# First mixer blocks summed in two halves, six blocks in step with the modulation, heads between the later halves, and the mixer's loads moved further ahead

## The chip, the cores and the metric

The kernel runs on one core of a Trainium2 chip. The metric is the device time of one execution in microseconds; the median of three executions of the kernel before is 3031.77 us (3027.84 to 3035.3). Everything is one program on five engines that run side by side: TensorE (PE, with its weight loads PEld), VectorE (DVE), ScalarE (ACT), GpSimd (POOL) and SyncE (SP, which only issues transfers).

## What is computed

The reference is a block with a mixer and a product-key lookup, followed by two further layers. The change lies in the mixer, and here in its first part:

```python
mod = silu(c) @ w_ada + b_ada                 # six vectors: shift1, scale1, gate1, shift2, scale2, gate2
h = rms_norm(x, norm1_gain) * (1 + scale1) + shift1
p = h @ w_in                                  # [256, 2048] @ [2048, ...], K = 2048 in 16 chunks of 128
# fq, fk, fv, ff, mq, mk, mv, mo, mi, mf = split(p)
# fox_attention: 8 heads of 128 over 256 rows, logits + F[t] - F[s], causal softmax
# mlstm_chunkwise: 4 heads of 256 on silu(conv(mq, mk)), gates from mi, mf
y = concat([fox_out, mlstm_out]) @ w_out
```

All of it is fp32: a product is made of three matmuls of split operands (high by high, high by low, low by high), so each loaded weight block of 128 x 1024 is split by an ACT cast (`hi`, line 233) and a DVE subtraction (`lo`, line 234) before PE may use it.

## The kernel before

x has 256 rows; its transpose `hT` holds 16 chunks of 128 channels. A weight load (`load`, lines 228 to 235) fetches 512 KB into a buffer `raw` by a transfer that SP issues, and splits it into `hi` and `lo`. In the mixer there are six `raw` buffers and three each of `hi` and `lo`. A block of `gemm_a` (lines 260 to 273) is 512 columns wide: eight loads, each followed by 12 matmuls of 512 columns (lines 249 to 251). `gemm_b` (lines 275 to 287) gives the transposed product, with lines 257 and 258. Sums of both go to the PSUM tag `mm` (four buffers, two to a block); everything else in PSUM uses the tag `at` (four buffers).

**The loop over the modulation** (lines 477 to 486) has eight rounds of two chunks. A round loads four 1 MB blocks of `w_ada` (`aw`, eight buffers), reduces each on DVE to a column of shift or scale (`ada_dot`, line 373), modulates and transposes two chunks of x into `hT`, and runs one load each of the first three blocks of `w_in` (q, k and v of the first four attention heads): 36 matmuls. The sums of these blocks stay in PSUM through all eight rounds: two tiles each for q, k (tag `mm`) and v (tag `at`).

**The attention part** (lines 495 to 507) goes twice over q, k, v of four heads. `fox_qk` normalises and transposes q and k; `mx_gates` (once) makes the forget gates and sends them by two transfers of POOL's queue through DRAM to all partitions (`spread`, lines 624 to 631: `FB` for the attention heads, `MB` for the mLSTM heads). `fox_head` (lines 715 to 740) is a chain: two logit matmuls (723), POOL's addend `fadd` (724), a DVE row maximum (707), ACT's exponential (709), a DVE scaling (727), three transposes (731), an ACT copy, the product with v (736 to 738), the split of the result. The second pair's three blocks (24 loads) are written behind the first four heads and fill PE while these run.

**Then** the pools of the attention are closed, the pools of the mLSTM part are opened on the same memory, and `mx_conv` runs `gemm_b` twice for each of q and k; its sums leave PSUM through `joined` (lines 300 to 303) into tiles `cx` of the new pools. The rest of `w_ada` for the mixer (48 blocks, `ada_beside`, two buffers) is loaded and reduced beside these products, one generator step for each load of a product.

The order of each engine is made by the framework's list scheduler from program order. `soon()` moves a load, its cast and its subtraction ahead by `OFFM` places in that order (100); inside the modulation loop this is off (`self.ahead`). Buffers of one tag are handed out in program order.

Of the kernel before, what the change touches and what calls it, by code (L numbers as in the profile page):

```python
# [9 lines left out]
F32 = mybir.dt.float32  # L10
# [9 lines left out]
P = 128  # L20
S = 256
D = 2048
NK = 16
# [6 lines left out]
X2=1  # L30
X3=0
PR=2
OFFM = 100
OFFP = 130
OFFA = 100
OFFB = 80
# [128 lines left out]
class K:  # L165
# [91 lines left out]
        mm(out, wh, x, start=start, stop=False)  # L257
        mm(out[:, 0, :], wl, x[:, 0, :], start=False, stop=stop)  # L258

    def gemm_a(self, xT, w, off, nk, width, out=None, part=None):  # L260

        xh, xl = xT[:2]
        out = out or [self.ps([P, width], "mm") for _ in range(2)]
        per = max(1, min(nk, SUB // width))
        for c0 in part or range(0, nk, per):
            hi, lo = self.load(w, off + c0 * width, per * width)
            for c in range(c0, c0 + per):
                s = slice((c - c0) * width, (c - c0 + 1) * width)
                for t in range(2):
                    tt = slice(t * P, t * P + P)  # L270
                    self.mm3(out[t], xh[:, c, tt], xl[:, c, tt], hi[:, s], lo[:, s], c == 0, c == nk - 1)
            self.step()
        return out

# [172 lines left out]
    def mixer(self, x_in, xd):  # L447

        nc, tc, a = self.nc, self.tc, self.a
        wctx = ExitStack()  # L450
        self.wpools(wctx, 2, 1, 1, "right")
        ctx = ExitStack()
        hT = self.xt_tiles(self.pool(ctx, "mxh", 1))
        sm = self.pool(ctx, "mxs", 1)
        mk = sm.tile([P, 7 * P], F32, name="mxmask")
        self.tri = mk[:, 0:P]
        self.cmask = mk[:, P:4 * P]
        self.cmask_t = mk[:, 4 * P:7 * P]
        pre = ExitStack()
        xp = self.pool(pre, "mxx", 1)  # L460
        x = xp.tile([P, 2, D], F32, name="x0")
# [10 lines left out]
        self.row_scale(xp, ss, r)  # L472
        off = NK * 16
        W = NK * 512
        first = [[self.ps([P, 512], tag) for _ in range(2)] for tag in ("mm", "mm", "at")]
        self.ahead = False
        for c in range(0, NK, 2):
            ws = [(vec, k, self.ada_load(vec, k)) for vec in range(2) for k in (c, c + 1)]
            for w in ws:
                self.ada_dot(*w)  # L480
            for vec in range(2):
                self.ada_fix(vec, c, 2)
            part = range(c, c + 2, 2)
            self.modulated(x, r, 0, hT, part)
            for i in range(3):
                self.gemm_a(hT, a["w_in"], off + i * W, NK, 512, first[i], part)
        self.ahead = True
        pre.close()
        oT = self.xt_tiles(self.pool(wctx, "mxo", 1, "right"))
        self.ada_open(wctx, 2, "right")  # L490
        self.side = self.ada_beside((2, 4, 3))
        fox = ExitStack()
        at = fox.enter_context(tc.tile_pool(name="mxa", bufs=2))
        a1 = fox.enter_context(tc.tile_pool(name="mxb", bufs=1))
        for g in range(2):
            qT = self.fox_qk(a1, at, hT, off, "fq", -(128.0 ** -0.5), first[0])
            kT = self.fox_qk(a1, at, hT, off + W, "fk", 1.0, first[1])
            ps = first[2] or self.gemm_a(hT, a["w_in"], off + 2 * W, NK, 512)
            v = at.tile([P, 2, 512], F32, tag="fv", name=self.nm("fv"))
            for t in range(2):  # L500
                nc.scalar.copy(v[:, t, :], ps[t])
            first = [None] * 3
            if g == 0:
                gates = self.mx_gates(sm, a1, hT)
            off += 3 * W
            for h in range(4):
                self.fox_head(at, gates, qT, kT, v, g * 4 + h, h, oT)
        fox.close()
        at = fox.enter_context(tc.tile_pool(name="mxc", bufs=2))
        a1 = fox.enter_context(tc.tile_pool(name="mxd", bufs=1))  # L510
        pend = []
        for g in range(2):
            qT = self.mx_conv(at, hT, off, g * 4, "mq")
# [74 lines left out]
    def mx_gates(self, p, fox, hT):  # L588
# [32 lines left out]
            mm(t[:, P:S], lf[:, 1], self.tri, start=False, stop=True)  # L621
            return t

        def spread(pool, x, name):

            n = x.shape[0]
            d = self.dp.tile([1, n * S], F32, name=name + "d")
            nc.gpsimd.dma_start(d.rearrange("o (n q) -> (o n) q", n=n), x)
            out = pool.tile([P, n, S], F32, name=name)
            nc.gpsimd.dma_start(out.rearrange("p n q -> p (n q)"), d.to_broadcast([P, n * S]))  # L630
            return out


        FL = fox.tile([8, S], F32, name="gFL")
        nc.vector.tensor_copy(FL, rows(lf[:, :, 0:8]))
        FB = spread(fox, FL, "gFB")
        fr = fox.tile([4, S], F32, name="gfr")
        nc.vector.tensor_copy(fr, rows(lf[:, :, 8:12]))
        ir = self.ps([4, S])
# [3 lines left out]
        nc.vector.tensor_sub(ar, ir, fr)  # L643
        M = fox.tile([4, S], F32, name="gM")
        nc.vector.tensor_tensor_scan(M, ar, ar, 0.0, op0=OP.max, op1=OP.max)
        negM = fox.tile([4, S], F32, name="gnegM")
        nc.vector.tensor_scalar(negM, M, -1.0, None, op0=OP.mult)
        MB = spread(p, negM, "gMB")
        negm = fox.tile([4, S], F32, name="gnegm")
        nc.vector.tensor_sub(negm, negM, fr)  # L650
        pm = self.ps([P, 2, 4])
# [6 lines left out]
    def head_norm(self, pool, ps, nh, hd, out, dim, rs=None):  # L658


        nc = self.nc
        ss = pool.tile([P, 2, nh], F32, tag="hn_ss", name=self.nm("hss"))
        for t in range(2):
            sq = pool.tile([P, nh * hd], F32, tag="hn_sq", name=self.nm("hsq"))
            nc.scalar.activation(sq, ps[t][:, :nh * hd], AF.Square, scale=1.0 if rs is None else rs[:, t:t + 1])
            nc.vector.tensor_reduce(ss[:, t, :], sq.rearrange("p (h d) -> p h d", h=nh), axis=AX.X, op=OP.add)
        r = pool.tile([P, 2, nh], F32, tag="hn_r", name=self.nm("hr"))
        self.rsqrt(r, ss, 1.0 / dim)
        if rs is not None:
            nc.vector.tensor_mul(r, r, rs.unsqueeze(2).to_broadcast([P, 2, nh]))  # L670
        for t in range(2):
            nc.vector.tensor_mul(
                out[:, t, :].rearrange("p (h d) -> p h d", h=nh),
                ps[t][:, :nh * hd].rearrange("p (h d) -> p h d", h=nh),
                r[:, t, :].unsqueeze(2).to_broadcast([P, nh, hd]))

    def fox_qk(self, a1, at, hT, off, gname, scale, ps):

        nc = self.nc
        ps = ps or self.gemm_a(hT, self.a["w_in"], off, NK, 512)  # L680
        n = a1.tile([P, 2, 512], F32, tag="fqn", name=self.nm("fqn"))
        self.head_norm(at, ps, 4, P, n, P)
        g = self.col(gname)
        if scale != 1.0:
            gs = at.tile([P, 1], F32, tag="gs", name=self.nm("gs"))
            nc.vector.tensor_scalar(gs, g, scale, None, op0=OP.mult)
            g = gs
        out = at.tile([P, 4, S], F32, tag="t" + gname, name=self.nm("fT"))
        for h in range(0, 4, 2):
            t = self.ps([P, 2, S])  # L690
            for i in range(2):
                for k in range(2):
# [767 lines left out]
```

## Time and profile before

| | us |
|---|---|
| median of three executions | 3031.77 |
| profiled execution | 3031.14 |
| its span in the trace | 3029.4 |
| PE busy in the span | 2929.3 (97%) |
| DVE busy | 2275.2 (75%) |
| ACT busy | 1665.4 (55%) |
| from the start to the last matmul of the modulation loop | 142.4 |
| to the end of the last attention head | 268 |
| to the end of the mixer, about | 540 |

Matmul records overlap, since PE takes the next one before the last has drained; a busy PE is therefore not a PE at its peak, and the distance between two starts is what a matmul costs. The mixer is the first sixth of the span.

### The profile page before, as it was taken

Reading aid. Unit: us, or ns where it says so; the run is one execution under the profiler, and the core shown is the slowest. Engines: PE = TensorE matmul, PEld = TensorE weight load, DVE = VectorE, ACT = ScalarE, POOL = GpSimd, SP = SyncE. Lnnn points to the kernel's source line nnn. Section 1 sums busy time; section 2 is a strip of 40 time slices with the busy share of each in tenths; the row PEclk is TensorE's granted clock in tenths of the full one; section 3 lists DMA queues with packets and bytes.
Section 4 is the critical chain, followed back from the end, with each engine's and each line's share of the span. In section 5 each row is a group of like instructions: output and inputs, shape, how many; then the busy total and the mean of one; then the engine's idle time right before and its main releaser. Section 6 shows DMA issues by size and latency. Waiting matters only on the chain.

```text
span 3029.4 us, 41563 instructions
## 1 busy us (share of the span) xinstructions
PE 2929.3 (97%) x14698; PEld 2441.4 (81%) x14698; DVE 2275.2 (75%) x3863; ACT 1665.4 (55%) x2696; POOL 194.1 (6%) x228
## 2 busy tenths in 40 slices
PE   5899999899999999999999999999999999999998
PEld 4578888688888888888688878887878888888877
DVE  6888985799789999656765677777688865666664
ACT  4455654444555555454444456666567755655662
POOL 0021000000000000532700000000000000000000
PEclk9899999899999999999999999999999999999999
DMA  9888996675666666776766666666544466555555
GB/s 399 335 313 316 329 342 207 253 284 179 197 193 216 218 215 219 254 237 227 250 195 190 193 196 190 194 193 197 181 133 136 136 207 196 167 175 170 165 166 160
DMA packets 172870, 660.45 MB, mean 218 GB/s; under 512 B 20071, under 2 KB 21107, under 8 KB 159731
## 3 DMA queue, kind: packets, MB, share of 16 engines
q1 hardware_dynamic: 152640, 604.70, 60.0%
q0 software_dynamic: 10368, 37.24, 3.6%
q10 hardware_dynamic: 9654, 15.85, 1.6%
q8 instruction: 115, 1.88, 0.3%
q14 instruction: 93, 0.76, 0.1%
HBM read 632.54 MB, written 25.18 MB: 217 GB/s over the span
## 4 chain that ended last, share of the span: by engine, by line
PE 90%; DVE 5%; ACT 3%; issue 1%; DMA 1%; ACTq 0%; POOL 0%; DVEq 0%; SPq 0%
PE ps L257 23%; PE ps L250 17%; PE ps L249 17%; PE ps L251 17%; PE ps L258 12%; DVE aw L373 2%; DVE lo L234 2%; ACT hi L233 1%; PE ps L862 1%; PE ps L335 0%; PE ps L359 0%; PE ps L1126 0%; ACT v L440 0%; PE ps L992 0%; DMA sB<-in_crow_dram 0%
## 5 line engine op out<-in xcount | busy, mean ns | idle before, releaser
L234 DVE TENSOR_TENSOR lo<-raw,hi 128x1024 fp32r<-128x1024 f32 x962 | 1191.0, 1241 | 515.4 <-ACT hi L233 426.0
L233 ACT CAST hi<-raw 128x1024 fp32r<-128x1024 f32 x962 | 1001.0, 1044 | 692.7 <-PE ps L251 258.0
L257 PE MATMUL ps<-xT,hi 128*128 128x512 f32 (+1 forms) x3104 | 1105.8, 398 | 17.5 <-ACT hi L233 10.5
L258 PE MATMUL ps<-xT,lo 128*128 128x256 f32 (+1 forms) x3104 | 874.6, 283 | 2.0 <-DVE lo L234 1.8
L257 PEld LDWEIGHTS ps<-xT,hi 128*128 128x128 f32 (+1 forms) x3104 | 582.2, 188 | 150.7 <-ACT hr L317 12.0
L258 PEld LDWEIGHTS ps<-xT,lo 128*128 128x128 f32 (+1 forms) x3104 | 585.6, 189 | 7.8 <-DVE lo L234 3.9
L249 PE MATMUL ps<-hi,xT 128*128 128x512 f32 x1152 | 463.8, 404 | 15.0 <-ACT xT L441 11.8
L250 PE MATMUL ps<-lo,xT 128*128 128x512 f32 x1152 | 463.2, 402 | 2.8 <-DVE lo L234 2.5
L251 PE MATMUL ps<-hi,xT 128*128 128x512 f32 x1152 | 462.9, 402 | 0.0
L250 PE MATMUL ps<-lo,wh 128*128 128x512 f32 x1024 | 402.8, 393 | 7.5 <-DVE lo L234 7.5
L249 PE MATMUL ps<-hi,wh 128*128 128x512 f32 x1024 | 403.0, 394 | 1.2 <-ACT wh L306 1.0
L251 PE MATMUL ps<-hi,wl 128*128 128x512 f32 x1024 | 400.2, 392 | 1.3 <-DVE wl L307 1.2
L306 ACT CAST wh<-R 128x256 fp32r<-128x256 f32 x384 | 155.4, 406 | 307.8 <-PE ps L250 301.2
L249 PEld LDWEIGHTS ps<-hi,xT 128*128 128x128 f32 x1152 | 220.9, 192 | 65.4 <-ACT xT L441 13.2
L250 PEld LDWEIGHTS ps<-lo,xT 128*128 128x128 f32 x1152 | 221.7, 192 | 53.2 <-DVE lo L234 5.3
L251 PEld LDWEIGHTS ps<-hi,xT 128*128 128x128 f32 x1152 | 220.8, 192 | 50.3 <-DVE xT L442 0.5
L307 DVE TENSOR_TENSOR wl<-R,wh 128x256 fp32r<-128x256 f32 x384 | 168.3, 440 | 100.2 <-ACT wh L306 99.1
L373 DVE CUSTOM_DVE_ANT_0 aw<-aw,sB 128x2048 f32<-128x2048 f32 x96 | 220.0, 2305 | 25.2 <-ACT sB L360 20.2
L250 PEld LDWEIGHTS ps<-lo,wh 128*128 128x128 f32 x1024 | 192.4, 188 | 55.5 <-DVE lo L234 14.7
L251 PEld LDWEIGHTS ps<-hi,wl 128*128 128x128 f32 x1024 | 191.9, 188 | 45.9 <-DVE wl L307 3.5
L249 PEld LDWEIGHTS ps<-hi,wh 128*128 128x128 f32 x1024 | 192.5, 188 | 43.7 <-ACT wh L306 2.0
L877 POOL TENSOR_TENSOR R<-R,gld 128x256 f32<-128x256 f32 (+1 forms) x96 | 111.1, 1171 | 51.6 <-DMA gld<-gd 51.1
(369 smaller groups left out, 2367.6 us busy)
## 6 DMA issues: line engine op xcount, KB each, us to landing
raw<-in_down_dram SPq DMA_DIRECT2D x256, 512.0 KB, 3.6
raw<-in_up_dram SPq DMA_DIRECT2D x256, 512.0 KB, 3.6
aw<-in_w_ada_dram SPq DMA_DIRECT2D x96, 1024.0 KB, 7.9
raw<-in_b_in_dram SPq DMA_DIRECT2D x128, 512.0 KB, 3.5
raw<-in_w_in_dram SPq DMA_DIRECT2D x112, 512.0 KB, 6.0
raw<-in_a_in_dram SPq DMA_DIRECT2D x49, 512.0 KB, 3.5
raw<-in_w_out_dram SPq DMA_DIRECT2D x32, 512.0 KB, 4.2
raw<-in_w_query_dram SPq DMA_DIRECT2D x32, 512.0 KB, 5.6
```

The source lines that it names most:

```text
L233: self.nc.scalar.copy(hi[:, :n], raw)
L234: self.nc.vector.tensor_sub(lo[:, :n], raw, hi[:, :n].bitcast(F32))
L249: mm(out, lh, rh, start=start, stop=False)
L250: mm(out, lh, rl, start=False, stop=False)
L251: mm(out, ll, rh, start=False, stop=stop)
L257: mm(out, wh, x, start=start, stop=False)
L258: mm(out[:, 0, :], wl, x[:, 0, :], start=False, stop=stop)
L306: self.nc.scalar.copy(hi, src)
L307: self.nc.vector.tensor_sub(lo, src, hi.bitcast(F32))
L373: nc.vector.tensor_tensor_reduce(out=w, in0=w, in1=self.sB, scale=1.0, scalar=0.0, op0=OP.mult, op1=OP.add, accum_out=out)
L862: mm(ps[:, k, :], o2[:, i + k, :], o1[:, i + k].rearrange("p a n -> p (a n)"), start=True, stop=True)
L877: nc.gpsimd.tensor_mul(d, d, st[:, cuts[i] - n0:cuts[i + 1] - n0, :])
```

## The change

Three things move. The first three blocks of `w_in` are summed in two halves: rounds 0 to 3 make chunks 0 to 7, whose sums ACT copies into a new tile `half` in SBUF (12 KB per partition). Rounds 4 to 7 then run six loads each: chunks 8 to 15 of the second three blocks, and chunks 0 to 7 of the same blocks from the `hT` that is already there, so that q, k, v of heads 4 to 7 are complete with the loop. What is left, chunks 8 to 15 of the first three blocks (12 loads), is run behind the gates, one block each ahead of heads 4, 5 and 6; DVE adds each to its `half`. Then q and k of heads 0 to 3 are normalised, and heads 7, 0, 1, 2, 3 follow. `OFFM` goes from 100 to 250. To make room, the mixer has five `raw` buffers, the broadcast of `MB` moves into the mLSTM's pool behind the attention, `negM` shares the tile of `M`, and the square buffer `hn_sq` of `head_norm` has one buffer everywhere (two before in the two later layers).

```diff
-OFFM = 100
+OFFM = 250
...
-    def gemm_a(self, xT, w, off, nk, width, out=None, part=None):
+    def gemm_a(self, xT, w, off, nk, width, out=None, part=None, ends=None):
+        a, b = ends or (0, nk - 1)
...
-                    self.mm3(out[t], xh[:, c, tt], xl[:, c, tt], hi[:, s], lo[:, s], c == 0, c == nk - 1)
+                    self.mm3(out[t], xh[:, c, tt], xl[:, c, tt], hi[:, s], lo[:, s], c == a, c == b)
...
-        self.wpools(wctx, 2, 1, 1, "right")
+        self.wpools(wctx, 1, 1, 1, "right")
...
+        half = sm.tile([P, 3, 2, 512], F32, name="half")
...
-        first = [[self.ps([P, 512], tag) for _ in range(2)] for tag in ("mm", "mm", "at")]
+        first = None
...
             self.modulated(x, r, 0, hT, part)
+            g = c // 8
+            if c % 8 == 0:
+                first = [[self.ps([P, 512], tag) for _ in range(2)] for tag in ("mm", "mm", "at")]
             for i in range(3):
-                self.gemm_a(hT, a["w_in"], off + i * W, NK, 512, first[i], part)
+                self.gemm_a(hT, a["w_in"], off + (3 * g + i) * W, NK, 512, first[i], part, (8, -1) if g else (0, 7))
+            for i in range(3 * g):
+                b = range(c - 8, c - 6, 2)
+                self.gemm_a(hT, a["w_in"], off + (3 + i) * W, NK, 512, first[i], b, (-1, 7))
+            if c == 6:
+                for i in range(3):
+                    for t in range(2):
+                        nc.scalar.copy(half[:, i, t, :], first[i][t])
...
-        for g in range(2):
-            qT = self.fox_qk(a1, at, hT, off, "fq", -(128.0 ** -0.5), first[0])
-            kT = self.fox_qk(a1, at, hT, off + W, "fk", 1.0, first[1])
-            ps = first[2] or self.gemm_a(hT, a["w_in"], off + 2 * W, NK, 512)
...
-            if g == 0:
-                gates = self.mx_gates(sm, a1, hT)
-            off += 3 * W
-            for h in range(4):
-                self.fox_head(at, gates, qT, kT, v, g * 4 + h, h, oT)
+        qkv = fox_qkv(first)
+        gates = self.mx_gates(sm, a1, hT)
+        rest = []
+        for i in range(3):
+            ps = self.gemm_a(hT, a["w_in"], off + i * W, NK, 512, None, range(8, NK, 2), (8, NK - 1))
+            for t in range(2):
+                nc.vector.tensor_add(half[:, i, t, :], ps[t], half[:, i, t, :])
+            rest.append([half[:, i, t, :] for t in range(2)])
+            self.fox_head(at, gates, *qkv, 4 + i, i, oT)
+        old, qkv = qkv, fox_qkv(rest)
+        self.fox_head(at, gates, *old, 7, 3, oT)
+        for h in range(4):
+            self.fox_head(at, gates, *qkv, h, h, oT)
+        off += 6 * W
...
+        gates["MB"] = gates["MB"](a1)
...
-            sq = pool.tile([P, nh * hd], F32, tag="hn_sq", name=self.nm("hsq"))
+            sq = pool.tile([P, nh * hd], F32, tag="hn_sq", name=self.nm("hsq"), bufs=1)
```

`fox_qkv(ps)` is the old body of the loop up to the copy of v, for sums that are handed in; `spread` now returns a function that makes the second transfer when it is called.

## Rows read from the trace of the kernel before

**Rows 1.** Busy time by stretch: length, then engine busy us (instructions), granted clock, DMA share, GB/s.
```profile
core 0: us, PE busy (x) PEld busy (x) DVE busy (x) ACT busy (x) POOL busy (x), PEclk, DMA share, GB/s
...
88.80:142.40 53.60, 42.47 (x153) 32.91 (x152) 49.43 (x63) 21.45 (x35) 0.00 (x0) 0.84 0.86 344
...
238.30:268.30 30.00, 29.77 (x180) 25.73 (x179) 26.20 (x50) 16.95 (x35) 4.27 (x4) 1.00 0.86 313
...
340.00:540.00 200.00, 195.88 (x932) 162.62 (x930) 151.69 (x196) 103.03 (x151) 0.00 (x0) 1.00 0.80 283
```

**Rows 2.** DVE in order of time, one round: start us, us, then instruction [idle before].
```profile
87.29 1.23 DVE L234 TENSOR_TENSOR lo<-raw,hi 128x1024 fp32r<-128x1024 f32 x1
...
90.03 2.36 DVE L234 TENSOR_TENSOR lo<-raw,hi 128x1024 fp32r<-128x1024 f32 x2 [0.49 <-ACT hi L233]
92.31 2.28 DVE L373 CUSTOM_DVE_ANT_0 aw<-aw,sB 128x2048 f32<-128x2048 f32 x1
...
101.77 1.23 DVE L234 TENSOR_TENSOR lo<-raw,hi 128x1024 fp32r<-128x1024 f32 x1
```

**Rows 3.** PE in order of time, in the last round of the loop and behind it.
```profile
134.31 0.63 PE L250 MATMUL ps<-lo,xT 128*128 128x512 f32 x1
134.73 0.63 PE L251 MATMUL ps<-hi,xT 128*128 128x512 f32 x1
...
138.33 0.39 PE L250 MATMUL ps<-lo,xT 128*128 128x512 f32 x1
138.56 0.39 PE L251 MATMUL ps<-hi,xT 128*128 128x512 f32 x1
...
142.37 1.55 PE L359 MATMUL ps<-sB,cst 1*128 1x512 f32 x3
```

**Rows 4.** Transfers of the first 120 us: all of them, and the weight loads (landing).
```profile
DMA packets 8944, 48.64 MB, mean 405 GB/s; under 512 B 1116, under 2 KB 1500, under 8 KB 4586
...
raw<-in_w_in_dram SPq DMA_DIRECT2D x24, 512.0 KB, 15.0
```

**Rows 5.** POOL in order of time: the first addend of a head.
```profile
180.65 1.53 POOL L724 TENSOR_TENSOR fadd<-mxmask,gFB 128x128 f32<-128x128 f32 x1 [6.85 <-ACT hi L233]
```

**Rows 6.** PE in order of time: logits (L723) of heads, transposes of q and k (L693).
```profile
174.17 0.92 PE L723 MATMUL ps<-fT,fT 128*128 128x128 f32 x4
...
191.42 0.82 PE L723 MATMUL ps<-fT,fT 128*128 128x128 f32 x4
...
202.06 0.82 PE L723 MATMUL ps<-fT,fT 128*128 128x128 f32 x4
...
210.92 0.82 PE L723 MATMUL ps<-fT,fT 128*128 128x128 f32 x4
...
217.01 1.04 PE L693 MATMUL ps<-cst,fqn 128*128 128x128 f32 x8
221.84 0.38 PE L693 MATMUL ps<-cst,fqn 128*128 128x128 f32 x2
...
238.28 0.82 PE L723 MATMUL ps<-fT,fT 128*128 128x128 f32 x4
...
261.33 0.82 PE L723 MATMUL ps<-fT,fT 128*128 128x128 f32 x4
```

**Rows 7.** ACT in order of time, between the first and the second head.
```profile
192.19 1.28 ACT L317 ACT_TABLE_LOAD   x1
193.48 0.30 ACT L317 ACTIVATE hr<-hss,eps 128x8 f32<-128x8 f32 x1
```

**Rows 8.** PE's groups between 238.6 and 268.2 us: count, busy us, mean ns.
```profile
L257 PE MATMUL ps<-xT,hi 128*128 128x512 f32 x64 | 23.4, 400 | 0.0
```

**Rows 9.** PE and POOL in order of time, behind the last attention head.
```profile
270.21 0.50 PE L257 MATMUL ps<-xT,hi 128*128 128x512 f32 x1 [1.55 <-DVE cx L303]
...
268.42 4.22 POOL L767 TENSOR_TENSOR me<-gMB,mxmask 128x256 f32<-128x256 f32 x4 [18.88 <-PE ps L738]
```

**Rows 10.** Who waited for whom on PE, 600 us to the end: total, times, longest.
```profile
PE ps L257 <- DVE qn L672: 3.4, 1, 3.4
```

More of the change, by code (lines that the diff above doesn't have):

```diff
@@ L494, in mixer, with fox_qkv @@
         a1 = fox.enter_context(tc.tile_pool(name="mxb", bufs=1))
-        for g in range(2):
-            qT = self.fox_qk(a1, at, hT, off, "fq", -(128.0 ** -0.5), first[0])
-            kT = self.fox_qk(a1, at, hT, off + W, "fk", 1.0, first[1])
-            ps = first[2] or self.gemm_a(hT, a["w_in"], off + 2 * W, NK, 512)
+        def fox_qkv(ps):
+            qT = self.fox_qk(a1, at, "fq", -(128.0 ** -0.5), ps[0])
+            kT = self.fox_qk(a1, at, "fk", 1.0, ps[1])
             v = at.tile([P, 2, 512], F32, tag="fv", name=self.nm("fv"))
             for t in range(2):
-                nc.scalar.copy(v[:, t, :], ps[t])
-            first = [None] * 3
-            if g == 0:
-                gates = self.mx_gates(sm, a1, hT)
-            off += 3 * W
-            for h in range(4):
-                self.fox_head(at, gates, qT, kT, v, g * 4 + h, h, oT)
+                nc.scalar.copy(v[:, t, :], ps[2][t])
+            return qT, kT, v
+        qkv = fox_qkv(first)
[12 more added lines that the diff above has]
+        off += 6 * W
         fox.close()
@@ L622, in rows, with spread @@
             return t
-        def spread(pool, x, name):
+        def spread(x, name):
             n = x.shape[0]
@@ L628, in spread, with get @@
             nc.gpsimd.dma_start(d.rearrange("o (n q) -> (o n) q", n=n), x)
-            out = pool.tile([P, n, S], F32, name=name)
-            nc.gpsimd.dma_start(out.rearrange("p n q -> p (n q)"), d.to_broadcast([P, n * S]))
-            return out
+            def get(pool):
+                out = pool.tile([P, n, S], F32, name=name)
+                nc.gpsimd.dma_start(out.rearrange("p n q -> p (n q)"), d.to_broadcast([P, n * S]))
+                return out
+            return get
         FL = fox.tile([8, S], F32, name="gFL")
         nc.vector.tensor_copy(FL, rows(lf[:, :, 0:8]))
-        FB = spread(fox, FL, "gFB")
+        FB = spread(FL, "gFB")(fox)
         fr = fox.tile([4, S], F32, name="gfr")
@@ L645, in mx_gates @@
         nc.vector.tensor_tensor_scan(M, ar, ar, 0.0, op0=OP.max, op1=OP.max)
-        negM = fox.tile([4, S], F32, name="gnegM")
+        negM = M
         nc.vector.tensor_scalar(negM, M, -1.0, None, op0=OP.mult)
-        MB = spread(p, negM, "gMB")
+        MB = spread(negM, "gMB")
         negm = fox.tile([4, S], F32, name="gnegm")
@@ L675, in head_norm, with fox_qk @@
                 r[:, t, :].unsqueeze(2).to_broadcast([P, nh, hd]))
-    def fox_qk(self, a1, at, hT, off, gname, scale, ps):
+    def fox_qk(self, a1, at, gname, scale, ps):
         nc = self.nc
-        ps = ps or self.gemm_a(hT, self.a["w_in"], off, NK, 512)
         n = a1.tile([P, 2, 512], F32, tag="fqn", name=self.nm("fqn"))
```

## The prediction

> **What bounds the kernel now.** I read the busy time by stretch first, then the list of PE's instructions in order of time over the mixer, then the other engines at the places where PE stood. The reader should see three regimes. In the modulation loop PE has gaps: in its second half it is busy 42.47 of 53.6 us at a mean granted clock of 0.84, while DVE is busy 49.43 [rows 1]. A round is 14.48 us long on DVE, from subtraction to subtraction (87.29 to 101.77); from 92.31 to 101.77 it makes the four reductions and their small repairs, 9.46 us, and two subtractions behind each other take 90.03 to 92.31, 1.14 each [rows 2]. So DVE sets the round, and the transfers stand close behind: 405 GB/s on the mean of the first 120 us [rows 4], and a round wants 5.5 MiB, 5.77 MB, 14.2 us. PE needs much less: a matmul of 512 columns starts 0.23 us after the one before it at full clock (138.33 to 138.56) and 0.42 at half (134.31 to 134.73) [rows 3]; 36 of them are 8.3 us.
>
> Behind the loop PE is nearly full: 29.77 of 30 us under the last four heads, 195.88 of 200 from 340 us on [rows 1]. The heads do not stop it, though they are a strict chain. The logits of the next head always come directly behind the product with v of the head before: heads start at 174.17, 191.42, 202.06, 210.92, and the transposes of the next q and k at 217.01 [rows 6]. Nothing of a head overlaps with the next; the buffers of the tag `at` are handed out in program order, and the next head's logits come behind this head's last tile. The chain costs nothing as long as PE has blocks to run beside it. It runs out of them at one place: PE makes exactly 64 matmuls of line 257 under heads 4 to 7 [rows 8], which is two `gemm_b` of 32, all that the four `mm` buffers hold, and then stands 1.55 us until `cx` is written [rows 9]. `cx` lies in a pool on the attention's memory, and that memory comes free with the last head: POOL's first mLSTM addend waited 18.88 us for that head's product [rows 9]. **The end of the last head, 268.2 us, is a gate** behind which everything later starts; today PE reaches it 1.9 us early.
>
> **The change part by part.** Rounds 0 to 3 keep their work. The six copies into `half` go to ACT, which is idle 32 of the 53.6 us that follow [rows 1]; the first block is complete a third into its last round. If that cover is gone PE waits for one pair of buffers. I take 0.5 us, between 0 and 2.
>
> Rounds 4 to 7 gain three loads each. DVE: three subtractions of 1.14, so 14.48 + 3.42 = 17.9 us. Transfers: 7 MiB, 7.34 MB at 405 GB/s, 18.1 us. PE: 72 matmuls at 0.23, 16.6 us, and four transposes. All three come out almost equal, and they hang on each other through three `hi` and `lo` buffers; I take 18.5. The lower end is DVE's 17.9. The upper end comes from the five `raw` buffers: a load lands after 15.0 us [rows 4], cast and subtraction hold it about 2.5 more, so five in 17.5 us, and six take 21.0. The loop now ends at 142.4 [rows 3]. Three rounds grow by 4.0 (12.0 us) and the last has 36 matmuls more (8.3): 162.7. Ends: 3 x 3.4 + 8.3, less up to 2.5 for matmuls that no longer run at half clock, gives 158.4; 3 x 6.5 + 8.3 gives 170.2.
>
> Taken away later: 12 loads of 12 matmuls at 0.23, 33.3 us of PE. If PE were all that counts, the gain would be 33.3 - 20.3 = 13.0 us.
>
> But the gate moves too. Counted from the loop's end, the first head ended at 191.42 - 142.37 = 49.05 us; what it waited for was the chain gates, DRAM, all partitions, whose first addend starts at 180.65 [rows 5]. Neither the gate product nor this chain is touched, so head 4 ends at 162.7 + 49.05 = 211.7. Seven heads then follow without a break, for their q and k are there or come early. The price of one: the fastest of before took 6.1 (210.92 to 217.01), the slowest 10.6 (191.42 to 202.06), and six of them (191.42 to 217.01 and 238.28 to 261.33) 8.1 on the mean [rows 6]. Heads 5 and 6 still run beside blocks: 7.5 each, 226.7. Then come the transposes of q and k of heads 0 to 3, which stand ahead of head 7 in the `at` order: 6.3 us before (217.01 to about 223.3), where the second group waited for its norm; 2.5 if nothing waits; I take 4.5, since this norm can be made early: 231.2. Head 7 at 7.0 and four at 6.5, nearest to the fastest because PE, out of blocks, asks for no casts: **the gate is at 264.2 instead of 268.2, 4.0 us earlier**. PE meanwhile runs dry. From 142.4 to 268.4 it now makes 24 loads (66.5 us), two `gemm_b` (64 times 0.23 and 64 halves, 22.2), waits some 3, and spends the other 34 us on heads, gates and transposes; after the change that is 33.3 + 22.2 + 34 = 89.5 from 162.7, until 252. The last 12 us ahead of the gate are empty.
>
> That emptiness has a price: behind gaps of 3 to 4 us the loop's matmuls ran at half clock for some microseconds, at 0.42 instead of 0.23 [rows 3], and the heads' own matmuls too. I take 2.0 us, between 0 and 4. The 1.9 us wait behind the gate remains.
>
> In a list: the six half sums on DVE lie under the blocks of heads 4 to 6, 0. The `MB` transfer leaves POOL's queue ahead of the first heads and enters it behind the last, ahead of the mLSTM addends, which are needed only after six more products; 0. One `hn_sq` buffer: the second square of each norm waits for the first reduction, some 0.7 us, and PE was seen to wait for such a norm once, 3.4 us [rows 10]; 0.7, between 0 and 5.6 if eight layers' norms come into the open. One `raw` less and `OFFM` 250 behind the gate: PE is full there with transfers at 0.80 [rows 1]; 0, within 2 either way. The rest of `w_ada` runs beside 108 loads instead of 120 and needs 96 of them, so it still ends before the mixer does, with 1 MiB per load's 2.8 us, 375 GB/s, under the 405 of [rows 4]; 0. The casts that `OFFM` moves go past the heads' steps on ACT and DVE: that is in the price of a head, and a rival below.
>
> Sum: -4.0 + 0.5 + 2.0 + 0.7 = -0.8 us, made against the profiled execution, 3031.14 (span 3029.4 and 1.7 around it): 3030.3. The median of the runs is 0.6 above that execution. I say 3030.
>
> A load of ACT's function table between a root and an exponential took 1.28 us, and the next activation started right behind it, 192.19 to 193.48 [rows 7]. The Trainium skill (ScalarE: Activation LUTs, What ACT_TABLE_LOAD costs) puts a switch of table at about 2.66 us, a load and as much again of drain. The trace shows only the load. By the page, and with the four switches of the new q and k norms in the chain, the sum would be 5.5 us higher.
>
> **The rivals.** *PE alone counts* (0.29): the memory behind the gate comes free earlier than I think, or heads go faster than any of before, and PE never runs dry. For it: PE is nearly full everywhere behind the loop [rows 1]. Against it: the stop after exactly 64 [rows 8] and POOL's wait [rows 9]. Then -13.0 + 1.2 = -11.8, about 3019; with rounds at 17.9, 3016. This is the outcome by the Trainium skill's rule (Perfetto Trace Analysis, Optimization Strategy) that regimes with different most-contended engines may gain by being interleaved. The rows agree that the loop and the stretch behind it are such regimes.
>
> *The heads go slower, and the gate later* (0.25): with `OFFM` at 250 casts and subtractions stand ahead of the heads' steps on ACT and DVE, and reductions of 2.28 us keep running between them. At 8.5 us a head and 6.3 for the transposes the gate is at 162.7 + 49.05 + 59.5 + 6.3 = 277.6, 9.4 later, and with 3.2 beside it the kernel takes 3044. It decides from 8.0 us a head on; the mean before was 8.1, against it that PE asks for fewer casts.
>
> *The loop does not take the blocks* (0.11): five `raw` buffers hold the round at 21.0; the loop ends at 170.2, the gate is at 271.7, and the sum is +6.7: 3038. That is the case in which the change doesn't do what it says.
>
> **How the numbers follow.** My own forecast has 0.35. Its range by itself is 3022 to 3039, from the ends of round and head price. With the rivals 8 in 10 lie from 3016 to 3044. A difference under 0.3%, 9.1 us, is about what a measurement of this kernel cannot tell from none: the forecast and the third rival fall inside it (0.46), the first gives faster (0.29), the second slower (0.25).
>
> **What would show it.** In the changed kernel's list of PE, the loop's last matmul should lie at 159 to 170 us; rounds 4 to 7 should be 18 to 19 us apart on DVE. Head 4's product with v should end some 49 us later, and each head's logits should stand directly behind the previous head's product. PE should have idle time of some 12 us in the heads 0 to 3, after 64 matmuls of line 257, ended by `cx`. If PE runs more than two `gemm_b` ahead of the last head, the gate is wrong and the first rival is right. If the last head ends past 274, the second is.

## The result and the profile after

The changed kernel takes 3056.43 us in the median of five executions (3055.21 to 3060.8), against 3031.77 before: 1.0086 times as long, with an interval of 1.0073 to 1.0100. The forecast was 3030 and no measurable difference. The profiled execution has a span of 3055.7 us, 26.3 more than before.

The marks below are starts in PE's list in order of time, in us. The end of the last head is the start of its last product: 267.8 in the kernel before, where the prediction counts from the end of that product, 268.2. "First block" is the first block of 512 columns behind the mLSTM's first products; its start is the first sign of what the stretch with the heads has won or lost.

| | before | forecast | after |
|---|---|---|---|
| end of the modulation loop | 142.4 | 162.7 | 171.6 |
| end of head 4 (before: the first head) | 191.4 | 211.7 | 221.7 |
| end of the last head | 267.8 | 264.2 | 286.6 |
| first block of 512 columns behind the heads | 294.8 | | 319.1 |

The busy time by stretch, after: length, then the engines' busy time and instructions, PE's granted clock, DMA share and GB/s. The first row is the loop's rounds 4 to 7, the second the last three heads, the third the same stretch as the last row of [rows 1].

```profile
core 0: us, PE busy (x) PEld busy (x) DVE busy (x) ACT busy (x) POOL busy (x), PEclk, DMA share, GB/s
88.10:171.60 83.50, 74.52 (x300) 58.51 (x300) 63.03 (x74) 34.54 (x49) 0.00 (x0) 0.94 0.83 329
...
262.70:286.60 23.90, 11.39 (x38) 7.57 (x38) 18.87 (x37) 5.51 (x18) 3.12 (x2) 0.50 0.67 238
...
340.00:540.00 200.00, 197.35 (x955) 164.24 (x954) 154.98 (x205) 109.01 (x171) 4.34 (x4) 1.00 0.84 295
```

In the loop no resource is full any more: DVE is busy 63 of 83.5 us where it had been busy 49 of 54 [rows 1]. Under the last three heads PE has nothing else to do, 38 instructions in 23.9 us, at half its clock. Later it is full again.

The heads, as logits (L751) in PE's order of time, with the transposes of q and k (L721) and the product that follows the last head:

```profile
208.68 0.92 PE L751 MATMUL ps<-fT,fT 128*128 128x128 f32 x4
...
221.67 0.82 PE L751 MATMUL ps<-fT,fT 128*128 128x128 f32 x4
...
231.97 0.82 PE L751 MATMUL ps<-fT,fT 128*128 128x128 f32 x4
...
241.84 1.04 PE L721 MATMUL ps<-cst,fqn 128*128 128x128 f32 x8
...
243.99 0.82 PE L751 MATMUL ps<-fT,fT 128*128 128x128 f32 x4
...
253.78 0.82 PE L751 MATMUL ps<-fT,fT 128*128 128x128 f32 x4
...
262.69 1.49 PE L751 MATMUL ps<-fT,fT 128*128 128x128 f32 x4
...
271.13 1.49 PE L751 MATMUL ps<-fT,fT 128*128 128x128 f32 x4
...
279.10 1.49 PE L751 MATMUL ps<-fT,fT 128*128 128x128 f32 x4
...
288.52 0.79 PE L257 MATMUL ps<-xT,hi 128*128 128x512 f32 x1 [1.25 <-DVE cx L305]
```

PE's group of line 257 from 222 to 288 us (count, busy us, mean ns, idle before):

```profile
L257 PE MATMUL ps<-xT,hi 128*128 128x512 f32 x64 | 23.0, 396 | 0.0
```

Head by head that is 10.3, 9.9, then 2.2 for the transposes, 9.8, 8.9, 8.4, 8.0 and 7.5 us. The picture is the forecast's: a strict chain, exactly 64 matmuls of line 257 beside it, then a stop until `cx` is there behind the last head. Its sizes are not.

### The profile page after: what moved, and what is told of

Its sections match the earlier page's. It is cut to its first block, busy times and chain, and to the rows that moved or that the text cites. A ratio compares the mean times of both kernels' runs of the same rounds, so it can differ in the third digit from the quotient of the medians.

```text
span 3055.7 us, 41568 instructions
## 1 busy us (share of the span) xinstructions
PE 2937.4 (96%) x14698; PEld 2445.9 (80%) x14698; DVE 2275.0 (74%) x3869; ACT 1671.7 (55%) x2704; POOL 191.5 (6%) x228
## 4 chain that ended last, share of the span: by engine, by line
PE 86%; DVE 6%; ACT 4%; issue 2%; DMA 2%; ACTq 0%; SPq 0%; DVEq 0%
PE ps L257 23%; PE ps L250 16%; PE ps L249 16%; PE ps L251 16%; PE ps L258 12%; DVE lo L234 3%; DVE aw L375 2%; ACT hi L233 2%; PE ps L890 1%; DMA aw<-in_w_ada_dram 1%; ACT p L737 1%; PE ps L337 1%; PE ps L361 0%; PE ps L1154 0%; ACT L737 0%
## 5 line engine op out<-in xcount | busy, mean ns | idle before, releaser
L257 PE MATMUL ps<-xT,hi 128*128 128x512 f32 (+1 forms) x3104 | 1107.7, 398 | 22.4 <-ACT hi L233 10.5
L249 PE MATMUL ps<-hi,xT 128*128 128x512 f32 x1152 | 462.2, 402 | 21.6 <-ACT xT L443 18.5
L917 ACT ACTIVATE R<-R 128x256 f32<-128x256 f32 x128 | 53.4, 418 | 106.3 <-DVE R L305 106.3
```

The costliest lines, as they stand in the source:

```text
L249: mm(out, lh, rh, start=start, stop=False)
L917: nc.scalar.activation(r, r, AF.Gelu)
```

## The experiments

The ratio is against the kernel before, measured beside it. The first three columns are the marks of the table above.

| run | loop end | last head ends | first block | median us | ratio |
|---|---|---|---|---|---|
| after | 171.6 | 286.6 | 319.1 | 3056.4 | 1.0086 [1.0073, 1.0100] |
| e1_offm100 | 169.2 | 278.3 | 304.6 | 3041.4 | 1.0030 [1.0015, 1.0046] |
| e7_before_offm250 | 141.3 | 276.7 | 307.6 | 3041.5 | 1.0042 [1.0026, 1.0059] |
| e4_dots_late | 170.8 | 255.8 | 295.2 | 3039.4 | 1.0023 [1.0011, 1.0034] |
| e3_cx_early | 171.0 | 290.7 | 300.7 | 3039.8 | 1.0030 [1.0018, 1.0043] |
| e6_mb_early | 172.0 | 288.3 | 318.7 | 3057.8 | 1.0096 [1.0078, 1.0114] |
| e8_offm100_cx_mb | 171.0 | 287.1 | 300.2 | 3046.4 | 1.0053 [1.0036, 1.0070] |
| e2_aw_ahead | 179.0 | 293.7 | 322.5 | 3062.1 | 1.0098 [1.0069, 1.0127] |
| e5_raw6 | 170.3 | 282.7 | 313.4 | 3054.7 | 1.0087 [1.0070, 1.0105] |
| e9_aw_mid | 174.0 | 280.9 | 306.9 | 3042.2 | 1.0042 [1.0025, 1.0059] |
| e11_dots_mid | 175.5 | 282.2 | 308.2 | 3048.2 | 1.0054 [1.0035, 1.0072] |
| e14_hi_lo_4 | 168.5 | 281.7 | 310.5 | 3050.6 | 1.0065 [1.0046, 1.0083] |
| e10_aw_mid_cx6 | 173.7 | 285.1 | 287.8 | 3026.3 | 0.9984 [0.9975, 0.9994] |
| e12_dots_mid_cx6 | 179.1 | 287.2 | 289.8 | 3032.8 | 0.9996 [0.9986, 1.0005] |
| e13_offm100_cx6 | 170.8 | 284.9 | 286.7 | 3025.2 | 0.9982 [0.9970, 0.9994] |
| e15_before_cx6 | 142.6 | 267.9 | 292.6 | 3027.0 | 0.9982 [0.9973, 0.9992] |

### The heads: OFFM, and the reductions beside them

```diff
-OFFM = 250
+OFFM = 100
```

> The changed kernel with OFFM back at 100, nothing else. Theory A (the casts that OFFM moves stand ahead of the heads' steps): the heads, 8.0 to 10.3 us each in the changed kernel, go back to about 7.5, the last head ends some 12 us earlier than 286.6, and the kernel takes about 3044. Theory B (the heads are slow because PE is out of blocks, its matmuls run at half clock, and reductions of w_ada stand between a head's steps): the order of casts does not matter, the last head ends within 3 us of 286.6, and the kernel takes 3053 to 3059.

The opposite edit, 100 to 250 alone in the kernel before:

> The kernel before with one part of the change alone: OFFM 250 instead of 100. Theory A: casts, subtractions and reductions that are ordered ahead of a head's steps lengthen each head wherever it stands; the last head of the kernel before then ends at 275 to 283 us instead of 268.2, and the time is 3038 to 3047. Theory B: the larger OFFM costs only where few blocks are left for PE beside the heads, as in the changed kernel; here the last head ends at 267 to 270, and the time is 3029 to 3034.

Both ways it is a large part of the loss of 24.7 us: 15.0 us less in the changed kernel, 12.5 more in the kernel before (3041.52 against 3029.05 beside it). It works in two places. The last head ends 8.3 us earlier in the one and 8.9 later in the other, and the way from there to the first block is 26.0 to 27.0 us at 100 (before, e1, e9, e11) and 28.8 to 32.5 at 250 (e2, e6, e5, e7, after). Of the 8.3 us, 2.4 lie already in the loop, and are not shown to be OFFM's: the same loop ended between 169.2 and 172.0 us in seven traces (after, e1, e3, e4, e6, e8, e13).

How a head gets longer stands in DVE's order of time, one head of the changed kernel and the corresponding one of e1:

```profile
264.54 0.42 DVE L735 CUSTOM_DVE_ANT_0 y<-ps,fadd 128x256 f32<-128x256 f32 x1
264.88 0.08 DVE L735 DVE_READ_ACCUMULATOR2_ANT m<- 128x1 f32 x1
264.88 2.29 DVE L375 CUSTOM_DVE_ANT_0 aw<-aw,sB 128x2048 f32<-128x2048 f32 x1
267.10 0.08 DVE L375 DVE_READ_ACCUMULATOR2_ANT av<- 128x1 f32 x1
267.10 0.16 DVE L739 RECIPROCAL m<-m 128x2 f32<-128x2 f32 x1
267.29 1.02 DVE L755 TENSOR_SCALAR p<-p,m 128x128 f32<-128x128 f32 x2
```
```profile
258.60 0.42 DVE L735 CUSTOM_DVE_ANT_0 y<-ps,fadd 128x256 f32<-128x256 f32 x1
...
258.94 1.22 DVE L234 TENSOR_TENSOR lo<-raw,hi 128x1024 fp32r<-128x1024 f32 x1
260.08 0.16 DVE L739 RECIPROCAL m<-m 128x2 f32<-128x2 f32 x1
260.27 1.03 DVE L755 TENSOR_SCALAR p<-p,m 128x128 f32<-128x128 f32 x2
261.23 2.28 DVE L375 CUSTOM_DVE_ANT_0 aw<-aw,sB 128x2048 f32<-128x2048 f32 x1
```

In the changed kernel a reduction of `aw` (2.29 us) stands between the row maximum and the reciprocal, although the exponentials of ACT, which the reciprocal needs, had ended by 265.7: 1.4 us of pure queue. So it is in heads 0 to 3 there; heads 5, 6 and 7 have a reduction between the row maximum and the scaling as well. In e1 it comes behind the scaling in heads 0 to 2. Head 2 makes a clean pair, for PE's granted clock is 0.50 in both: 8.0 us with the reduction inside (271.13 to 279.10 in PE's list of after), 6.6 without:

```profile
264.12 1.49 PE L751 MATMUL ps<-fT,fT 128*128 128x128 f32 x4
...
270.73 1.49 PE L751 MATMUL ps<-fT,fT 128*128 128x128 f32 x4
```

Head 3 has it inside in both kernels and takes 7.5 us in both. To see what the reductions cost in all, the next run begins them behind the heads:

```diff
-        self.ada_open(wctx, 2, "right")
-        self.side = self.ada_beside((2, 4, 3))
         fox = ExitStack()
...
         fox.close()
+        self.ada_open(wctx, 2, "right")
+        self.side = self.ada_beside((2, 4, 3))
```

> The changed kernel with the rest of w_ada (its buffers, its broadcast row and its reductions) begun only behind the last attention head. Theory A (a reduction of 2.2 us between a head's row maximum and its scaling delays the head by some 1.3 us each, and more where PE still has blocks): heads without blocks go from 8.0 to about 6.7 us, the others by 1 to 2 as well, the last head ends some 10 us earlier, at 276; what the later 96 reductions cost behind it, with no load left over, is up to 5 us; the kernel takes about 3050. Theory B (the heads wait for PE's half clock and their own chain alone): the last head ends within 3 us of 286.6 and the kernel takes 3056 or more.

The gain is larger than theory A said, and OFFM is still 250 here. PE's list, heads 0 to 3:

```profile
235.65 0.82 PE L751 MATMUL ps<-fT,fT 128*128 128x128 f32 x4
...
240.77 0.82 PE L751 MATMUL ps<-fT,fT 128*128 128x128 f32 x4
...
245.93 0.82 PE L751 MATMUL ps<-fT,fT 128*128 128x128 f32 x4
...
250.96 0.82 PE L751 MATMUL ps<-fT,fT 128*128 128x128 f32 x4
```

A head takes 5.1 us, less than the fastest of before (6.1), at full clock, and the last ends at 255.8, 12 us ahead of before. So a head's own steps are 5 us, and what made 7.5 to 10 of them is what DVE and ACT do in between and, in the last three heads, the clock: at 0.50 a head without a reduction inside took 6.6 us (e1, above). e4 takes both away together. But the first block starts at 295.2 and the whole kernel is 7 us slower than before: the 48 reductions now reach to 538 us instead of 455, and from 480 to 520 us the transfers move 396 GB/s where before they moved 218. The loss falls in that stretch: counted by the matmuls still to come, PE is 0.5 us behind the kernel before at its 340 us, and 9.3 behind at 520. The work under the heads was not free, and it isn't free later.

### The gate: cx, and the broadcast of MB

```diff
-            c = at.tile([P, S], F32, tag="cx", name=self.nm("cx"))
+            c = self.cxp.tile([P, S], F32, tag="cx", name=self.nm("cx"), bufs=4)
```

`cxp` is a pool that is open from the mixer's start (room: one buffer each for y, p and pt of the heads).

> The changed kernel with the tile cx of the convolutions in a pool that is open from the mixer's start (four buffers instead of two), so that two more products can leave PSUM before the attention's memory comes free; room for it comes from one buffer instead of two for three tiles of the heads. Theory A (the end of the last head is a gate only because PE has no place for a third product): PE makes 128 instead of 64 matmuls of line 257 ahead of the last head's end, the empty stretch of some 25 us there is filled with 22 us of products at full clock, and the kernel takes about 3034. Theory B (something else holds PE there, the weight loads or DVE): PE still stops after 64 and the kernel stays at 3056.

The broadcast, with the same room:

```diff
-        gates["MB"] = gates["MB"](a1)
...
-            MB = spread(negM, "gMB")
+            MB = spread(negM, "gMB")(p)
```

> The changed kernel with the MB broadcast made at its old place, beside FB's, ahead of the first head (room made as for the run with six raw buffers). Theory A: behind the last head ACT stands 4.49 us for POOL's me, which waits for this broadcast, and the hi casts of the products behind it stand with it; without that the first a-product of the mLSTM part starts 4 to 5 us earlier than 319.1 us, and the time is 3051 to 3053. Theory B: what follows the gate waits for its loads anyway; the a-product starts at 318 to 319, and the time is 3055 to 3058.

Both of these and OFFM 100, with v of heads 0 to 3 read from `half` for more room:

> The changed kernel with three suspected costs taken away together: OFFM 100, cx in a pool of its own that is there during the attention (four buffers), and the MB broadcast at its old place (room as before, and v of heads 0 to 3 read from half). Theory A: the three add up: heads shorter by about 8 us, the products with x no longer bound to the last head, no wait of ACT for MB; the first a-product starts at 287 to 293 us (294.8 in the kernel before, 300.7 with cx alone), and the time is 3024 to 3031. Theory B: the late loop end holds everything behind it, and what the first two give is the same time twice; the a-product starts at 296 to 301, and the time is 3035 to 3040.

The gate is real: with `cx` out of the attention's memory PE runs 128 matmuls of line 257 before the heads end, the first block starts 18.4 us earlier though the last head ends 4 us later, and 16.6 us are won. (The 15.0, 17.0 and 16.6 us of e1, e4 and e3 can't be added; they take away parts of the same loss of 24.7.) The broadcast of `MB`, which in the trace of after looks like a cause (ACT stands 4.49 us for POOL's `me`), is none: made early, it takes 2 us from the way behind the last head, the heads end 1.7 later, and the time is the same. Theory B was right there.

The run with all three was neither A nor B: 3046, slower than e1 or e3 alone. Its PE waits, 285 to 302 us:

```profile
PE ps L249 <- DVE cx L305: 11.1, 1, 11.1
```

The four `cx` were full, and they come free with the convolution, which is written into the mLSTM's pools: the same gate, one step on. And the products beside the heads made these slow again (287.1 instead of e1's 278.3). With six buffers (`bufs=6` in the diff above) and OFFM 100 that wait is gone; e10 has the loop of e9 (below) beside it, e13 the changed kernel's own loop, and e15 is the kernel before with the six buffers alone (room for them as in e8, in e15 as in e3):

> The kernel of the run with OFFM 100 and the aw in the middle, and beside it cx in a pool of its own with six buffers (four let the first four products with x run beside the heads, and then the next block of 512 columns waited 11.1 us for cx, which came free with the convolution behind the last head). Theory A: with two buffers more nothing of PE's waits for the last head any more; the first block of 512 columns starts within 3 us of the end of the products ahead of it, at 285 to 293 us, and the time is 3022 to 3031, PE alone being the bound. Theory B: DVE is what bounds the stretch from the loop to the mixer's middle (29.2 to 29.8 us busy of 30 in the run with four buffers), so PE stands elsewhere in it; the block starts at 294 to 300, and the time is 3034 to 3042.

> The changed kernel with OFFM 100 and six cx buffers in a pool that is there during the attention; the loop is the changed kernel's own. Against the run that had the aw transfers in the middle as well (loop end 173.7 us, 3026.3) only the loop differs. Theory A: with the gate gone PE's work is the bound and the loop's end counts in full: loop end 169 to 171, time 3021 to 3025. Theory B: DVE's stretch behind the loop hides these microseconds: time 3026 to 3029.

> The kernel before with six cx buffers in a pool that is there during the attention, and nothing else of the change. Theory A: before the change the last head costs PE 1.9 us only, so there is little to free: 3027 to 3031; what the version with halves, OFFM 100 and six cx buffers gained over the kernel before is then due to the halves. Theory B: a product more beside the heads gives as much here: 3019 to 3026.

With OFFM 100 and six `cx` the halves are no loss: 3025.2, 0.9982 of the kernel before. But six `cx` without any of the change give the same ratio, so the gain over the kernel before can't be put down to the halves. The two medians are 1.8 us apart, and those of e13 and e10, whose loop ends 2.9 later, 1.1: less than the intervals can tell, so theories A and B of e13 stay undecided by its time. Its first block starts 1.1 us ahead of e10's. The busy time from 200 to 320 us, first e13, then e15:

```profile
200.00:320.00 120.00, 118.39 (x629) 98.80 (x628) 116.10 (x190) 77.63 (x142) 30.50 (x26) 1.00 0.86 310
```
```profile
200.00:320.00 120.00, 117.99 (x613) 97.83 (x612) 109.88 (x163) 70.63 (x118) 16.32 (x14) 1.00 0.88 313
```

PE is full in both. In e13 DVE nearly is too, 116.1 of 120 us: in this stretch it has hardly any room left for the subtractions of more blocks beside the reductions.

### The loop: what makes a round 21.7 us

In the changed kernel the rounds begin on PE at 88.3, 110.7, 132.4 and 153.9. (With the same loop e1's begin at 87.2, 110.8, 132.2 and 152.3; the round from the third mark is 20.0 us there.) What ends PE's wait ahead of each is the transposed chunk of x; here the row for the third, then SP's transfers and DVE's order in the round before it:

```profile
132.40 0.79 PE L249 MATMUL ps<-hi,xT 128*128 128x512 f32 x1 [2.83 <-ACT xT L443]
```
```profile
110.68 1.86 SPq L368 DMA_DIRECT2D aw<-in_w_ada_dram  x4
113.17 19.32 SPq L222 DMA_DIRECT2D raw<-in_w_in_dram  x6
```
```profile
119.21 1.23 DVE L234 TENSOR_TENSOR lo<-raw,hi 128x1024 fp32r<-128x1024 f32 x1 [1.64 <-ACT hi L233]
120.36 2.28 DVE L375 CUSTOM_DVE_ANT_0 aw<-aw,sB 128x2048 f32<-128x2048 f32 x1
...
122.57 1.22 DVE L234 TENSOR_TENSOR lo<-raw,hi 128x1024 fp32r<-128x1024 f32 x1
...
128.32 2.29 DVE L375 CUSTOM_DVE_ANT_0 aw<-aw,sB 128x2048 f32<-128x2048 f32 x1
```

A round is a circle and not three resources side by side: PE's first matmul at 110.7; the fifth subtraction at 119.2, which waits for a cast, which waits for a `hi` buffer that PE frees; only then the four reductions, with the sixth subtraction among them, to 130.6; repairs, modulation, and PE again at 132.4. Five edits tried to open it:

```diff
+        nxt = [(vec, k, self.ada_load(vec, k)) for vec in range(2) for k in (0, 1)]
         for c in range(0, NK, 2):
-            ws = [(vec, k, self.ada_load(vec, k)) for vec in range(2) for k in (c, c + 1)]
+            ws = nxt
+            if c + 2 < NK:
+                nxt = [(vec, k, self.ada_load(vec, k)) for vec in range(2) for k in (c + 2, c + 3)]
```

> The changed kernel, in whose modulation loop the four w_ada blocks of the next round are issued ahead of this round's weight loads instead of behind them. Theory A (SP's order: the next round's w_ada blocks stand behind the sixth weight load, which waits for a raw buffer, and DVE then stands idle for want of reductions): rounds 4 to 7 shrink from 21.7 us to about 18.5, the loop ends at about 162 instead of 171, the last head ends as much earlier, and the kernel takes about 3047. Theory B (the three hi and lo buffers hold the round, whatever SP does): rounds stay at 21 to 22 and the kernel at 3056.

```diff
-        self.wpools(wctx, 1, 1, 1, "right")
+        self.wpools(wctx, 2, 1, 1, "right")
```

> The changed kernel with six raw buffers again instead of five (room made by one buffer each for y, p and pt of the attention heads, which follow one another strictly). Theory A: in rounds 4 to 7 the sixth raw transfer waits for a buffer, and the next round's aw transfers stand behind it in SP's queue; with six buffers the rounds go from 21.7 us to about 18.5, the loop ends at 160 to 164 us instead of 171.6, everything behind it moves with it, and the time is 3046 to 3050. Theory B: the round is a closed circle of casts, subtractions and matmuls through three hi and three lo buffers and of the modulation's wait for the reductions; a sixth raw buffer changes the loop's end by less than 2 us, and the time is 3054 to 3058.

The other three are edits of e1 (the last with the room of e8). In e9 the line that makes `nxt` stands between the three loads of new chunks and the three of old ones, in rounds 4 to 6 alone.

> The changed kernel with OFFM 100 and, in rounds 4 to 6 of the loop, the next round's four aw transfers issued behind the third of the six weight loads instead of behind the sixth; the comparison is with OFFM 100 alone (loop end 169.2 us, last head 278.3, 3041.4). Theory A: the round of 21.7 us is some 17.5 us of matmuls and some 4 us in which PE waits for the transposed chunks of x, because the reductions that make them start only when the aw transfers, queued behind six loads that wait for buffers, have landed; with the transfers in the middle the rounds are 18 to 19.5 us apart, as the late rounds were (18.6) when all rounds issued their aw ahead, the loop ends at 161 to 165, the last head at 270 to 275, and the time is 3033 to 3038. Theory B: the wait only moves to the loads that now stand behind the aw; the rounds stay at 21 to 22, the loop ends at 168 to 171, and the time is 3040 to 3044.

e11, where the third and fourth reduction and their `ada_fix` stand one load further on:

```diff
+                if early and i == 1:
+                    for w in nxt[:2]:
+                        self.ada_dot(*w)
...
+                if early and i == 1:
+                    self.modulated(x, r, 0, hT, range(c + 2, c + 4, 2))
...
+            if 8 <= c < NK - 4:
+                nxt = aw(c + 4)
```

> The changed kernel with OFFM 100 and the modulation one round ahead in rounds 4 to 6: the next round's four reductions stand in program order behind the second and the fourth weight load of a round, its modulation and transposes behind the fifth, its aw transfers a round earlier. Theory A: the round of 21.8 us is a circle through DVE's queue: PE's first matmul, 9.8 us to the fifth subtraction (whose cast waits for a hi buffer that PE frees), four reductions and a subtraction behind it (10.3), repairs, modulation and transposes (1.7), PE again; with the reductions ahead of the waiting subtractions the rounds 5 to 7 fall to 17.5 to 19.5 us, the loop ends at 158 to 165 instead of 169.2, and the time is 3031 to 3037 (OFFM 100 alone 3041.4). Theory B: matmuls, casts and transfers hold the round by themselves; the rounds stay above 20.5, the loop ends at 168 to 174, and the time is 3039 to 3044.

```diff
-        self.wpools(wctx, 1, 1, 1, "right")
+        self.wpools(wctx, 0, 2, 2, "right")
```

> The changed kernel with OFFM 100 and four hi and four lo buffers instead of three, and four raw instead of five for the room (a sixth raw had moved the loop's end by 1.3 us). The comparison is with OFFM 100 alone (loop end 169.2, 3041.4). Theory A: the fifth subtraction of a round waits for a cast that waits for a buffer that PE frees, and the reductions stand behind it; with one buffer more it waits for one load less, 2.8 us, so rounds 5 to 7 go to 18 to 19.5 us, the loop ends at 160 to 165, and the time is 3033 to 3038. Theory B: the buffers of the split are not what closes the round, or four raw cost what they give; the loop ends at 168 to 174, and the time is 3039 to 3045.

The sixth `raw` buffer acquits the transfers. SP and DVE with six:

```profile
102.05 1.90 SPq L368 DMA_DIRECT2D aw<-in_w_ada_dram  x4
```
```profile
119.32 1.23 DVE L234 TENSOR_TENSOR lo<-raw,hi 128x1024 fp32r<-128x1024 f32 x1 [1.57 <-ACT hi L233]
120.46 2.28 DVE L375 CUSTOM_DVE_ANT_0 aw<-aw,sB 128x2048 f32<-128x2048 f32 x1
```

The `aw` transfers go 8.6 us earlier, and the first reduction starts 0.1 us later than without; the loop ends 1.3 us earlier, within the spread of the unchanged loop. The forecast's third rival, five `raw` buffers, had the round's size (21.0) and the wrong cause.

e11 put the reductions ahead of the waiting subtractions. PE's wait for x went away (10.2 us in after: 4.30 ahead of the matmul at 88.3, then 2.83 and 3.04), and this stood in its place:

```profile
PE ps L250 <- DVE lo L234: 9.8, 3, 5.3
```

The three late rounds took 58.4 us, as in e1 (117.1 to 175.5, and 110.8 to 169.2), and round 4 had lost 6 us to the transfers that now stood ahead of its weights. e2's late rounds were 18.6 us apart (123.1 to 179.0), the forecast's pitch, and its early ones had lost more than that. e9's were 21.1 and 22.1 us, as theory B had it, behind a first one of 25.5. In e14 the round behind 111.1 took 19.0 us, as theory A had it, but with four `raw` buffers ACT then stood 8.16 us for a weight load; the loop ended at 168.5, and the time, 3050.6, is above both theories. So the circle is shown in its parts, and each edit moves the wait on by one place; whether the loop can be had in 163 us was not found. The last run has e11's loop and six `cx`:

> The same order of the reductions, and cx in a pool of its own with six buffers; the comparison is with six cx buffers and the aw transfers in the middle of the round (loop end 173.7 us, 3026.3). Theory A: nothing of PE's waits for the last head, so that what the loop gains arrives at the end; loop end 158 to 165, time 3014 to 3021. Theory B: DVE bounds the stretch behind the loop (28.3 to 30.0 us busy of each 30 from 200 to 320), and an earlier loop end only lets PE wait there; time 3023 to 3029.

With the gate gone, the loop's end does not count in full. e12 ends it 5.4 us later than e10, and its first block starts 2.0 later; its median is 6.5 us above e10's, but the kernel before, measured beside each, was 2.9 us slower there too. Neither of its theories came out. Part of what goes missing is the clock: right behind the loop it was granted at 0.76 in e13 (170.9 to 184.9 us), 0.84 in e10 (173.7 to 184.5) and 1.00 in e12 (179.1 to 188.4).

## Why the prediction was wrong

The mechanism held: the last head is the gate, the heads are a chain, 64 matmuls run beside it, and `cx` ends the wait. Head 4 ended 50.0 us behind the loop's end (forecast 49.05 [rows 3, 6]). The sum failed in the sizes of three of its terms, all to the same side.

**The round, 18.5 us.** It was 21.7, and the loop ended at 171.6 instead of 162.7, 8.9 us late. The step took the largest of three resources and a little more. In the kernel before this was right, because PE's 8.3 us lay inside DVE's 14.48 [rows 2, 3] and any wait of PE's for x was hidden in them. With 72 matmuls PE's work is itself most of a round, and the way from its last free buffer over cast, subtraction, reductions and modulation comes on top. In the round from 110.7 us the matmuls took 18.4 us and not 16.6, for some of them, between 111.8 and 115.2 us, ran at a granted clock of 0.51; 2.83 more were the wait for x.

**A head, 7.5 to 6.5 us.** The seven heads behind head 4 took 62.8 us instead of 48.0, 14.8 late. The argument was that PE out of blocks asks for no casts. But the 2.28 us reductions [rows 2] do not depend on PE's blocks; they go on, and with OFFM at 250 they stand inside the head. OFFM is the smaller part of it: with the transposes, forecast at 52.5 us, this stretch took 65.0 in after, 60.9 at OFFM 100 (e1) and 44.2 without reductions and at full clock (e4). The emptiness that was priced at 2.0 us in all lay in the heads too, as their half clock. The nearest row for a price was not the fastest head of before but the mean, 8.1 [rows 6]. The transposes were cheaper than thought (2.2 for 4.5).

Together, 8.9 + 1.0 + 14.8 - 2.3 = 22.4: the gate at 286.6 and not 264.2.

**OFFM 250 and one `raw` less behind the gate, 0 within 2.** From the last head to the first block it took 32.5 us against 27.0. With five or six `raw` the runs at 250 show 28.8 to 32.5, those at 100 show 26.0 to 27.0; with four `raw` it was 28.8 at 100 (e14). So OFFM takes some 2 to 6 us that were costed at nothing, on the ground that PE is full there [rows 1]. Right behind the gate it is not: in the trace of after PE stands 4.30 us for `cx` at 306.2, and 2.9 to 3.4 us in e2, e5, e6 and e7; at 100 (before, e1, e9, e11) no wait for `cx` there is longer than 1.6. Beside it the move of `MB` was rightly costed at 0, though the trace seemed to contradict it.

So the gate came 18.8 us later than before instead of 4.0 earlier, and the way from it to the first block grew by 5.5: 24.3 of the 26.3 us between the spans lie ahead of the first block. Behind it, the one long wait for a norm of q grew from 3.4 [rows 10] to 4.3 us (4.3 in e1, e3, e4 and e13 too, 3.4 in e7 and e15): `hn_sq`, forecast at 0.7, was about right. The half copies, forecast at 0.5, show no wait of PE's ahead of round 4 but the one for x that was there before (4.30 us for 4.15). About 1.1 us was not separated.

**The rivals.** The second (heads at 8.5 us, OFFM as the cause) named what happened, at a mean of 9.0 a head, and the third had the loop's end at 170.2. Each had been priced alone, 3044 and 3038. They do not exclude each other: their excesses over the forecast, 14 and 8, give 3052 together. The range ended at the larger of the two. Its lower end, 3016, does not come out of its condition: with three rounds at 17.9 instead of 18.5 the 3019 become about 3017.5.

**PE alone** (3019, -11.8) was reached by no run, gate or not. With the gate away (e13 against e15) the loop's end is 28.2 us later and 33.3 us of PE's work are done in it: 5.1 us. The first block starts 5.9 us earlier, and the medians show 1.8. The Trainium skill (Perfetto Trace Analysis, Optimization Strategy) says that interleaving regimes with different most-contended engines may improve performance. Here the loop's regime was not DVE's alone: it was the chain between DVE, ACT and PE, and more of PE's work made that chain longer.

## What to carry to other kernels

Before work is moved into a stage with a free engine, follow one round of that stage as a circle through the in-order queues: what the engine frees, who waits for it, and what is queued behind that waiter. Free time that lies in series with such a circle can't be filled at the price of the work alone. And an offset that orders loads earlier puts other work into the middle of every latency chain that has no slack: price a chain by its mean with the neighbours it will have, and add the rivals that can come together.

## What the hardware showed beside that

Under the last three heads PE's granted clock was 0.50, the lower of its two levels (1.2 GHz), over 23.9 us in which it was busy 11.4: logits took 1.49 us instead of 0.82. With products beside the same heads (e4) it was 1.00, and they took 0.82. It fell within a stretch (253.8 to 262.7 us, 0.77 on the mean) in which PE, running out of products, was busy 4.3 of 8.9 us. So the emptier PE came with slower matmuls in the chain itself.

A transfer that is issued earlier is no sooner used: with six `raw` buffers instead of five, `aw` was issued 8.6 us earlier, and the first reduction behind it stood where it had stood (120.46 us for 120.36).
